# Attention blocks and norms ordered behind the in-projection products that are emitted ahead of them, and a longer counted time from transposes to values

## The chip, the cores and the metric

The kernel runs on one core of one Trainium2 chip. The metric is the device time of one execution in microseconds, the median of several runs. For the kernel before, three runs took 3193.33, 3194.68 and 3197.3 us, so the time before is 3194.68 us.

## The reference, cut to what matters

A trunk of two layers over 1024 frames of width 1024, in f32. Layer 0 mixes with RWKV-7 and gated DeltaNet heads and isn't touched by the change. Layer 1 mixes with chunked softmax attention of 16 heads of 64: each chunk of 64 frames attends to itself and the 8 chunks before it, with a bias by relative distance. Each layer ends with a squared-ReLU MLP and a gated per-layer embedding.

```python
qkv = (h @ w_qkv).reshape(bsz, seq, 3, C_HEADS, C_HEAD_DIM)
q = rmsnorm(qkv[:, :, 0], q_g) * (C_HEAD_DIM ** -0.5)
k = rmsnorm(qkv[:, :, 1], k_g)
...
s = jnp.einsum('bqhd,bkhd->bhqk', q_c, k_b).astype(jnp.float32) + bias
s = jnp.where(valid, s, -jnp.inf)
prob = jax.nn.softmax(s, -1).astype(v.dtype)
return jnp.einsum('bhqk,bkhd->bqhd', prob, v_b)
```

## The kernel before, in words

Matrices are kept as a high part and a remainder (the "split": ScalarE copies the high part in a rounded f32 type, VectorE subtracts to get the remainder), and products of high and low parts are summed on TensorE.

Attention is cut into 16 **steps**: 8 pairs of heads (pr) by 2 halves of 512 frames (hf). A step has four parts, each written as a Python generator that emits instructions and yields between them:

- `attn_in` (L1666), driven by `attn_ins` (L1597): four **in-projection products** into one of the two "dps" banks of PSUM, each of 24 matmuls of 384 columns (`dps<-wq`), three per `yield 0`. Each bank is copied out by ScalarE (qk at L1699, vs at L1703) and VectorE (vs at L1704). Then GpSimd squares (L1711), VectorE sums (L1712), takes a reciprocal square root in short instructions (L259 to L264) and scales q and k (L1715). When the 16 steps' products are out, the same generator goes on with the per-layer embedding's projection and with the output projection (`ple_proj`, `out_early`).
- `attn_norm` (L1718), driven by `attn_norms` (L1633): **norm transposes** of k and of q (`dps<-ident,qk`, L165, into "dps" banks), each followed by gains and split (L1737 to L1740).
- `attn_block` (L1745), four per step (2 heads by 2 blocks of 256 queries), driven by two copies of `attn_lane` (L1645) that draw from one list of jobs. A **block** makes for each of its two rows of queries a near score into one of two "sn" banks and a far score into the one "sf" bank; VectorE adds the bias and takes the maximum (L1795, L1803), ScalarE exponentiates (L1805, L1808) and scales by the reciprocal of the sum (L1812). Then it transposes the probabilities into one of two "pt" banks (L165), splits them into ptile (ScalarE L317, VectorE L318), and multiplies by the values into "po" (`po<-ptile,vs`). For each piece the value product with the high part comes first and that with the remainder second.

All four generators go through `run` (L123). It keeps a clock of its own, `now`, that matmuls and transposes advance (L151, L163), and for each generator a due time. It always resumes the first generator in its list that is due. A generator that yields a key such as "attn_block3" is due again after the time that the table `LAT` gives the key (L81 to L84); one that yields a tuple waits until another has marked it. The list is: two lanes, the norms, the in-projection. So the in-projection is resumed when nothing ahead of it in the list is due: it is the **filler**. It may run at most three steps ahead of the blocks (L1601).

What `run` makes is an order of emission. The framework then schedules: each engine's instructions are placed by priority (the order of emission) and by readiness in its own model of time, so an instruction that was emitted later can be placed ahead of one that the model holds to be not ready yet. The placed order of each engine is fixed in the program; on the chip each engine runs it in that order, with semaphores where it needs another engine's result.

Of the kernel before, what the change touches and what calls it, by code (L numbers as in the profile page):

```python
# [80 lines left out]
    "attn_block0": 0.97,  # L81
    "attn_block1": 4.45,
    "attn_block2": 0.43,
    "attn_block3": 0.94,  # L84
    "qk": 11.25,
    "norm": 1.28,
    "end_front": 46.33,
# [17 lines left out]
class Trunk:  # L105
    def __init__(self, ctx, tc, a, dbg=None, stop=None):
# [3 lines left out]
        self.now, self.done, self.lat = 0.0, {}, LAT  # L110
        self.nd, self.rx, self.late, self.extra = -1, None, None, []

    def dump(self, name, ap, idx=None):
        if name in self.dbg:
            d = self.dbg[name]
            d = d if idx is None else d[idx]
            self.nc.sync.dma_start(out=d, in_=ap)
# [2 lines left out]

    def run(self, lanes):  # L123
        state, self.done = [[g, 0.0, None] for g in lanes], {}
        while state:
            best = None
            for st in state:
                if st[2] is not None:
                    if st[2] not in self.done:
                        continue  # L130
                    st[1], st[2] = max(st[1], self.done[st[2]]), None
                if st[1] <= self.now:
                    best = st
                    break
                if best is None or st[1] < best[1]:
                    best = st
            self.now = max(self.now, best[1])
            try:
                r = next(best[0])
            except StopIteration:  # L140
                state.remove(best)
                continue
            if isinstance(r, tuple):
                best[2] = r
            else:
                best[1] = self.now + self.lat.get(r, 0.0)
# [4 lines left out]
    def mm(self, out, lhsT, rhs, start, stop):  # L151
        n, m = 1, 1
        for c in rhs.shape[1:]:
            n *= c
        for c in lhsT.shape[1:]:
            m *= c
        if rhs.dtype == F32:
            self.now += 2 * max(n / 1200, m * 0.0007)
        else:
            self.now += max(n / 2400, m * 0.00035)  # L160
        return self.nc.tensor.matmul(out, lhsT, rhs, start=start, stop=stop)  # L161

    def tr(self, out, in_, ident):  # L163
        self.now += 0.107
        return self.nc.tensor.transpose(out, in_, ident)  # L165

    def bank(self, shape=None):

# [1407 lines left out]
    def layer1_in(self):  # L1576
        nc, tc, a = self.nc, self.tc, self.a
        with ExitStack() as es:
            self.psm = es.enter_context(self.pool("psml1", space=PSUM))
            wp = self.wp = es.enter_context(self.pool("l1a", 2))  # L1580
            self.wr = es.enter_context(self.pool("l1wr", 2))
            self.w1 = es.enter_context(self.pool("l1w1"))
            l1 = es.enter_context(self.pool("l1", 2))
            self.sm = es.enter_context(self.pool("sml1", 2))
            self.yd = [[self.dr.tile([P, HB], F32, tag=f"yd{k}{hf}", name="yd") for hf in range(2)] for k in range(NK)]
            rbl = l1.tile([P, 16], F32, tag="rbl", name="rbl", bufs=1)
            nc.sync.dma_start(out=rbl, in_=a["rb_last"].rearrange("(o c) -> o c", o=1).broadcast_to((P, 16)))

            steps = [(pr, hf) for pr in range(8) for hf in range(2)]
            self.st = {}  # L1590

            self.ql = [[pool.tile([P, HB], F32R, tag=tag, name="Ql", bufs=1) for pool, tag in
                        ((self.accp, f"acc{e}"), (l1, f"Ql{e}"))] for e in range(2)]
            jobs = iter([(s, h, b) for s in range(16) for h in range(2) for b in range(2)])
            self.run([self.attn_lane(steps, jobs, l1, rbl) for _ in range(2)] + [self.attn_norms(steps, l1), self.attn_ins(steps, l1)])

    def attn_ins(self, steps, l1):  # L1597
        kv = {}
# [355 lines left out]
```

## Time and profile before

| what | us |
|---|---|
| median of 3 runs | 3194.68 |
| the profiled execution | 3200.01 |
| its span, first to last instruction | 3198.3 |
| layer 0 up to its dense stages | 0 to 969 |
| dense stages of layer 0 | 969 to 1770 |
| attention, products of the in-projection | 1770 to 2278 |
| attention's last blocks beside the next projections | 2278 to 2395 |
| dense stages of layer 1 | 2395 to 3198 |

The stages are read off the chain that ended last and the timeline. In the rows, PE is TensorE's matmul, PEld its weight load, DVE VectorE, ACT ScalarE, POOL GpSimd and SP SyncE, which issues the DMAs. A row of the timeline gives start, time from the first start to the last end, engine, line, operation, tiles (out<-in), shape and count of like instructions that follow each other; in brackets is the idle time of the engine just ahead, and what ended it. Matmuls overlap, so the time of one is read from start to start.

### The profile page before, as it was taken

To read this page: it belongs to the slowest core of one execution; us is meant where nothing else is said; L and a number is where in the kernel's file an instruction comes from. 1 tells how busy PE (TensorE), PEld (TensorE's weight loads), DVE (VectorE), ACT (ScalarE), POOL (GpSimd) and SP (SyncE) were. 2 spreads that over 40 slices of the span, in tenths; PEclk is the share of its full clock that TensorE was granted. 3 is DMA by queue.
4 is the path that set the end of the run, shared out by engine and by line. 5 is a ranking of instruction groups with operands and counts; after the bars stand their busy time and mean duration, and the time that the engine had idled before them with its cause. 6 is when DMAs were issued, how large, how long until landed. Compare 5 with 4: busy or idle time off the path is not lost.

```text
span 3198.3 us, 46044 instructions
## 1 busy us (share of the span) xinstructions
PE 3102.1 (97%) x17576; PEld 2565.6 (80%) x17576; DVE 2013.2 (63%) x4020; ACT 1384.2 (43%) x2608; POOL 531.5 (17%) x978
## 2 busy tenths in 40 slices
PE   7999999999999999999999898999899999999999
PEld 5777777777777888888888888988778888888887
DVE  6566675556748666655546576776768666655552
ACT  4333333334326555322123477777756555312121
POOL 6334442433410000000004211010110000000002
PEclk8999899999899999999999999999999999999999
DMA  3322112212325433523213210110156433522213
GB/s 120 94 63 60 47 46 67 70 61 70 129 95 194 155 119 108 192 93 106 92 51 128 70 36 32 45 41 16 69 177 209 150 121 109 185 105 92 106 47 105
DMA packets 144716, 309.60 MB, mean 97 GB/s; under 512 B 40944, under 2 KB 43120, under 8 KB 144496
## 3 DMA queue, kind: packets, MB, share of 16 engines
q1 hardware_dynamic: 126064, 273.10, 25.6%
q10 hardware_dynamic: 18432, 33.56, 2.7%
q8 instruction: 138, 2.26, 0.3%
q14 instruction: 82, 0.67, 0.1%
HBM read 232.16 MB, written 74.45 MB: 96 GB/s over the span
## 4 chain that ended last, share of the span: by engine, by line
PE 85%; DVE 7%; ACT 3%; DMA 2%; issue 1%; POOL 0%; SPq 0%; ACTq 0%; DVEq 0%; POOLq 0%
PE dps L161 70%; PE ch L161 3%; PE iz L161 2%; PE pm L161 2%; PE tp L161 1%; PE po L161 1%; PE py L161 1%; DVE ptile L318 1%; PE pt L165 1%; DMA wraw<-in_w_qkv 1%; PE sn L161 1%; PE pp L161 1%; DVE pb L1795 1%; PE sc L161 1%; ACT pb L1808 1%
## 5 line engine op out<-in xcount | busy, mean ns | idle before, releaser
L161 PE MATMUL dps<-r,act 128*128 128x512 f32 x3528 | 824.4, 392 | 0.0
L161 PEld LDWEIGHTS dps<-r,act 128*128 128x128 f32 x3528 | 662.1, 188 | 145.7
L161 PE MATMUL dps<-xg,whi 128*128 128x512 f32 x1280 | 438.2, 418 | 11.7 <-ACT xg L320 7.3
L161 PE MATMUL dps<-late,act 128*128 128x512 f32 x1536 | 352.9, 391 | 0.0
L161 PEld LDWEIGHTS dps<-late,act 128*128 128x128 f32 x1536 | 288.4, 188 | 63.1
L161 PE MATMUL dps<-wq,act 128*128 128x384 f32 x1536 | 304.8, 344 | 5.8 <-DVE vs L1704 3.1
L1452 POOL TENSOR_TENSOR pn<-pn,prs 128x512 f32<-128x512 f32 x32 | 45.5, 1426 | 1590.7 <-ACT prs L354 1496.3
L161 PEld LDWEIGHTS dps<-xg,whi 128*128 128x128 f32 x1280 | 248.4, 199 | 75.2 <-issue 10.7
L161 PEld LDWEIGHTS dps<-wq,act 128*128 128x128 f32 x1536 | 265.6, 191 | 10.4 <-DVE vs L1704 5.1
L161 PE MATMUL dps<-xg,wlo 128*128 128x512 f32 x640 | 266.4, 416 | 3.1 <-DVE wlo L277 3.1
L1328 DVE TENSOR_TENSOR late<-late,dps 128x512 f32<-128x512 f32 x224 | 152.9, 685 | 150.1 <-PE dps L161 119.2
L1427 DVE TENSOR_TENSOR xw<-xw,dps 128x512 f32<-128x512 f32 x192 | 131.5, 685 | 148.4 <-PE dps L161 145.5
L1226 ACT CAST act<-act 128x1024 fp32r<-128x1024 f32 (+1 forms) x99 | 94.8, 964 | 285.2 <-DMA act<-in_w 124.2
L1226 ACT CAST act<-late 128x512 fp32r<-128x512 f32 x210 | 124.5, 618 | 135.9 <-PE dps L161 117.0
L1227 DVE TENSOR_TENSOR act<-late,act 128x512 fp32r<-128x512 f32 x210 | 139.9, 687 | 26.1 <-ACT act L1226 25.9
L161 PEld LDWEIGHTS dps<-xg,wlo 128*128 128x128 f32 x640 | 126.9, 198 | 34.1 <-issue 4.8
L161 PE MATMUL dps<-xw,act 128*128 128x512 f32 x576 | 138.9, 392 | 0.0
L276 ACT CAST whi<-wraw 128x1024 fp32r<-128x1024 f32 x78 | 81.7, 1047 | 124.2 <-PE dps L161 74.4
L161 PEld LDWEIGHTS dps<-xw,act 128*128 128x128 f32 x576 | 108.1, 188 | 24.1
L1227 DVE TENSOR_TENSOR act<-act 128x1024 fp32r<-128x1024 f32 (+1 forms) x99 | 109.9, 1115 | 21.0 <-ACT act L1226 19.8
L161 PE MATMUL po<-ptile,vs 128*128 128x256 f32 (+1 forms) x576 | 104.9, 297 | 17.1 <-DVE ptile L318 7.7
L277 DVE TENSOR_TENSOR wlo<-wraw,whi 128x1024 fp32r<-128x1024 f32 x78 | 101.4, 1301 | 25.6 <-ACT whi L276 25.6
(472 smaller groups left out, 5369.4 us busy)
## 6 DMA issues: line engine op xcount, KB each, us to landing
act<-in_w SPq DMA_DIRECT2D x68, 512.0 KB
hd<-late ACTq DMA_DIRECT2D x128, 256.0 KB
late<-in_w SPq DMA_DIRECT2D x60, 512.0 KB
wraw<-in_w_in SPq DMA_DIRECT2D x56, 512.0 KB
act<-hd SPq DMA_DIRECT2D x56, 512.0 KB
wraw<-in_w_out SPq DMA_DIRECT2D x21, 512.0 KB
wraw<-in_w_qkv SPq DMA_DIRECT2D x21, 512.0 KB
pn<-pnd SPq DMA_DIRECT2D x32, 256.0 KB
```

What stands on the lines that cost most here:

```text
L161: return self.nc.tensor.matmul(out, lhsT, rhs, start=start, stop=stop)
L165: return self.nc.tensor.transpose(out, in_, ident)
L276: nc.scalar.copy(hi, raw)
L277: nc.vector.tensor_tensor(lo, raw, hi.bitcast(F32), op=ALU.subtract)
L318: nc.vector.tensor_tensor(dst[:, 1, sl], src, dst[:, 0, sl].bitcast(F32), op=ALU.subtract)
L1226: A.copy(hi, s)
L1227: V.tensor_tensor(lo, s, hi.bitcast(F32), op=ALU.subtract)
L1328: V.tensor_tensor(r, t, u, op=ALU.add)
L1427: V.tensor_tensor(x[n][:, sl], x[n][:, sl], ps, op=ALU.add)
L1452: G.tensor_tensor(pn, pn, prs[:, sl], op=ALU.mult)
L1795: V.tensor_tensor_reduce(S, pn[:, 0:nn * P], toep[:, (3 - nn) * P:], op0=ALU.add, op1=ALU.max, scale=1.0, scalar=NEG, accum_out=mx[:, 0:1])
L1808: A.activation(S, S, AF.Exp, bias=mx[:, 2:3], accum_out=l[:, 0:1])
```

## The change

Two edits. The table's time for "attn_block3", the yield between a block's last transposes and its value products, goes from 0.94 to 2.20. And `run` gets a flag, `behind`, that is set for attention alone. With it, every time a generator other than the last in the list (the filler) is resumed, the first matmul or transpose that it emits gets an edge to the last matmul that the filler has emitted: the scheduler may not place it ahead of that one. The edge is an order on TensorE itself and adds no semaphore. The filler's own instructions get no edge.

```diff
-    "attn_block3": 0.94,
+    "attn_block3": 2.20,
...
+        self.filled, self.step = None, "free"
...
-    def run(self, lanes):
+    def run(self, lanes, behind=False):
         state, self.done = [[g, 0.0, None] for g in lanes], {}
+        filling, self.filled = lanes[-1] if behind else None, None
...
             self.now = max(self.now, best[1])
+            self.step = "free" if not behind else "fill" if best[0] is filling else "tie"
             try:
                 r = next(best[0])
             except StopIteration:
                 state.remove(best)
                 continue
+            finally:
+                self.step = "free"
...
-        return self.nc.tensor.matmul(out, lhsT, rhs, start=start, stop=stop)
+        return self.placed(self.nc.tensor.matmul(out, lhsT, rhs, start=start, stop=stop))
+
+    def placed(self, ins):
+
+        if self.step == "fill":
+            self.filled = ins
+        elif self.step == "tie" and self.filled is not None:
+            self.tc.add_manual_dep(ins.ins, self.filled.ins.name, mybir.DependencyInfo(
+                mybir.DependencyClass.NoSync, mybir.DependencyReason.DATA), reason="order")
+            self.step = "tied"
+        return ins
...
-        return self.nc.tensor.transpose(out, in_, ident)
+        return self.placed(self.nc.tensor.transpose(out, in_, ident))
...
-            self.run([self.attn_lane(steps, jobs, l1, rbl) for _ in range(2)] + [self.attn_norms(steps, l1), self.attn_ins(steps, l1)])
+            self.run([self.attn_lane(steps, jobs, l1, rbl) for _ in range(2)] + [self.attn_norms(steps, l1), self.attn_ins(steps, l1)],
+                     behind=True)
```

## The prediction, made before the changed kernel ran

> **What bounds the kernel now.** I read the page's busy times first, then its chain, then the stages, then the waits of the one stage that the diff can reach.
>
> ```profile
> span 3198.3 us, 46044 instructions
> PE 3102.1 (97%) x17576; PEld 2565.6 (80%) x17576; DVE 2013.2 (63%) x4020; ACT 1384.2 (43%) x2608; POOL 531.5 (17%) x978
> ...
> PE 85%; DVE 7%; ACT 3%; DMA 2%; issue 1%; POOL 0%; SPq 0%; ACTq 0%; DVEq 0%; POOLq 0%
> ```
>
> TensorE is busy 97% of the span and is 85% of the chain that ended last. So only two things can move the time: gaps between matmuls, and the speed at which they run. The change touches the attention part of layer 1 alone, so the next view cuts the span by stage (time, PE, PEld, DVE, ACT, POOL busy, then the granted clock).
>
> ```profile
> 969.00:1770.00 801.00, 794.29 (x3478) 651.01 (x3478) 507.43 (x672) 307.74 (x467) 49.43 (x34) 0.99 0.36 124
> 1770.00:2278.00 508.00, 469.81 (x2939) 443.71 (x2940) 347.06 (x1136) 355.47 (x843) 56.70 (x64) 0.97 0.11 34
> ```
>
> In the dense stage ahead of it TensorE idles 6.7 us of 801. In attention it idles 508.00 - 469.81 = 38.2 us, with VectorE and ScalarE busy 68% and 70%: three engines hand work around, and TensorE runs out of something ready. The waits of TensorE in that stage and the tail of it (waiter, whom it waited for, total us, times, longest):
>
> ```profile
> PE po L161 <- DVE ptile L318: 7.7, 12, 1.6
> PE po L161 <- ACT ptile L317: 6.4, 10, 1.8
> PE dps L161 <- POOL acc L1465: 5.6, 1, 5.6
> PE pt L165 <- ACT pb L1812: 6.1, 9, 1.8
> PE pt L165 <- DVE ptile L318: 4.8, 12, 1.0
> PE sf L161 <- ACT pb L1805: 3.8, 7, 1.3
> PE dps L161 <- DVE vs L1704: 3.1, 6, 0.8
> ...
> PE dps L161 <- DVE F L1740: 1.8, 4, 0.5
> PE dps L165 <- DVE vs L1704: 1.7, 5, 0.5
> ```
>
> The largest family is the split of the transposed probabilities: value products wait for ptile (7.7 + 6.4), and new transposes wait until the split has emptied their bank (4.8), 18.9 us in all. Next come the transposes that wait for normalised probabilities (6.1), the two "dps" banks (3.1 + 1.8 + 1.7 = 6.6) and the one "sf" bank (3.8). The 5.6 us of acc is the start of the stage and lies ahead of the change. Where the waits sit shows in the timeline:
>
> ```profile
> 2081.28 0.55 PE L161 MATMUL po<-ptile,vs 128*128 128x128 f32 x3 [0.30 <-DVE ptile L318]
> 2081.67 0.63 PE L165 MATMUL pt<-ident,pb 128*128 128x128 f32 x4
> 2083.27 0.44 PE L165 MATMUL pt<-ident,pb 128*128 128x128 f32 x2 [0.97 <-DVE ptile L318]
> ...
> 2085.16 2.18 PE L161 MATMUL po<-ptile,vs 128*128 128x256 f32 x9 [0.92 <-DVE y L1854]
> 2087.14 0.63 PE L161 MATMUL sn<-F,F 128*128 128x384 f32 x1
> 2087.57 0.52 PE L161 MATMUL sn<-F,Ql 128*128 128x384 f32 x1
> ...
> 2098.17 3.57 PE L161 MATMUL dps<-wq,act 128*128 128x384 f32 x19
> ```
>
> From 2078.5 to 2098.2 no in-projection product runs: the blocks have only each other to hide behind. In this stretch three waits stand within 4 us, and right after them the matmuls slow down. The granted clock of such 25 us slices (third figure from the end):
>
> ```profile
> 1875.00:1900.00 25.00, 21.98 (x132) 19.72 (x132) 16.56 (x59) 20.56 (x54) 0.38 (x1) 0.93 0.03 11
> 1950.00:1975.00 25.00, 22.82 (x142) 21.33 (x141) 16.44 (x53) 18.46 (x45) 1.04 (x1) 0.93 0.03 11
> 1975.00:2000.00 25.00, 21.89 (x134) 20.69 (x133) 17.55 (x60) 17.95 (x42) 3.43 (x3) 0.93 0.06 19
> 2075.00:2100.00 25.00, 21.48 (x120) 19.19 (x119) 18.28 (x69) 17.56 (x48) 2.43 (x3) 0.80 0.16 53
> 2150.00:2175.00 25.00, 21.58 (x131) 19.25 (x129) 16.93 (x66) 17.97 (x47) 1.04 (x1) 0.93 0.16 53
> ```
>
> These five lose 25 x (4 x 0.07 + 0.20) = 12 us of clock. So the stage gives away about 38 + 12 = 50 us, 1.6% of the time, and that is all the change has to win.
>
> **The change, part by part.** No instruction is added or taken away, and no semaphore: the new edges only order TensorE's own instructions. Built, the two programs hold the same instructions on every engine. On TensorE the order is the same for the first 8,380 of 15,134 instructions and for the last 3,487; ScalarE, VectorE, GpSimd and SP also differ only inside attention. The diff alone doesn't tell the new order (a scheduler has the last word), so I counted in the two built orders. For a wait what matters is its **cover**: the TensorE work that stands between the matmul that starts a chain on the other engines and the matmul that needs its result. I price it from full-clock rows:
>
> ```profile
> 1850.02 0.36 PE L161 MATMUL sn<-F,F 128*128 128x384 f32 x1
> 1850.21 0.34 PE L161 MATMUL sn<-F,Ql 128*128 128x384 f32 x1
> ...
> 1851.64 4.43 PE L161 MATMUL dps<-wq,act 128*128 128x384 f32 x24
> 1855.91 0.28 PE L161 MATMUL sf<-F,F 128*128 128x256 f32 x1
> 1856.03 0.28 PE L161 MATMUL sf<-F,Ql 128*128 128x256 f32 x1
> ```
>
> Start to start, a product is 4.27 / 24 = 0.178 us, a 384-column score 0.19, the small ones 0.11 to 0.12 (I take 0.11).
>
> (1) *Transposes to values.* The later due time of attn_block3 (0.94 to 2.20) lets the lanes emit about 1.3 us more of products between a block's transposes and its values, and the new edges keep the scheduler from pulling the values ahead of them. The split costs at least
>
> ```profile
> L317 ACT CAST ptile<-pt 128x512 fp32r<-128x512 f32 (+2 forms) x117 | 57.2, 515 | 22.0 <-PE pt L165 21.0
> L318 DVE TENSOR_TENSOR ptile<-pt,ptile 128x512 fp32r<-128x512 f32 (+2 forms) x117 | 67.7, 594 | 11.2 <-ACT ptile L317 10.0
> ```
>
> 0.52 + 0.59 = 1.11 us, and more where it queues. Of the 144 splits, the cover up to the first value product that needs the low half is under 2.0 us 56 times before and 36 times after; what is missing to 2.0 us sums to 39.6 us before and 26.7 after. The ratio is 0.67 there, 0.67 with 1.5 us and 0.68 with 2.5 us, so it doesn't hang on the chain's length. The 18.9 us become 12.8: **-6.1 us**.
>
> (2) *Banks and normalised probabilities.* With block steps spread behind the products, the same count gives for the "dps" banks (chain taken as 2.0 us) 16.7 missing before and 8.9 after, half of 6.6: **-3.3**; it would be no gain at all if the chain were 3 us (39.4 and 39.9). For "sf" (2.0 us) 4.9 and 2.7: 45% of 3.8, **-1.7**. For the way from scores to transposes (5 us) 19.0 and 8.3: 56% of 6.1, **-3.4**. Sum of (1) and (2): -14.5 us of 38.2.
>
> A check by another count: the stretches of over 4 us of priced work without a product are 11 before (64.8 us, longest 10.3) and 10 after (51.6, longest 5.7). The longest, priced 10.3, took 19.6 us in the timeline above, 0.9 us lost per us. The 13.2 us fewer are then worth 12 us, waits and clock together: the same size.
>
> (3) *The clock.* If the halvings follow the waits, 14.5 / 38.2 = 38% of 12 us go: **-4.5**. The Trainium skill ("TensorE: Matmul & The Clock Gate", HAM oscillation) puts the rule as no idle gaps of TensorE over about 3.4 us. No wait here is that long (longest 1.8), and yet the clock halved, so the trace doesn't agree with it as a bound on single gaps; by that rule the term would be 0 and the forecast 4.5 us later. (A later section of that page names frequent short idles as another way to oscillation, which is nearer to these rows.)
>
> (4) *Norm transposes, moved forward.* This is what the change can cost. The transposes of q and k wait for a chain: copy, squares on GpSimd, sums, rsqrt, and a multiply on VectorE. Before, they stand behind 19 products of the next step; after, they stand ahead of them, at the end of the stretch without products. Seven of the sixteen have priced cover of 8.2 to 9.3 us (8.6 on average) instead of 12.0 to 13.8. Two of these in the trace, each the last product, the multiply and the transposes:
>
> ```profile
> 2107.36 4.43 PE L161 MATMUL dps<-wq,act 128*128 128x384 f32 x24
> ...
> 2121.33 1.23 DVE L1715 TENSOR_TENSOR qk<-qk,nn 128x1024 f32<-128x1024 f32 x1
> 2125.28 0.60 PE L165 MATMUL dps<-ident,qk 128*128 128x128 f32 x4
> 2246.72 1.72 PE L161 MATMUL dps<-wq,act 128*128 128x384 f32 x9
> 2256.69 1.23 DVE L1715 TENSOR_TENSOR qk<-qk,nn 128x1024 f32<-128x1024 f32 x1
> 2261.95 0.60 PE L165 MATMUL dps<-ident,qk 128*128 128x128 f32 x4
> ```
>
> The chain ended 2122.56 - 2111.79 = 10.8 and 2257.92 - 2248.44 = 9.5 us after the last product, with 2.7 and 4.0 us to spare. Against 8.6 us it would be late by 2.2 and 0.9, some 11 us over seven steps. But the cover is priced without waits; the stretch inside it loses time of its own (5.3 us at 0.9 per us is some 4 us more), and VectorE's order puts the multiply earlier too. Bounds: 0, and 11. I take **+2.5**, near the lower end, because cover in real time exceeds the chain.
>
> (5) *DMAs.* SP keeps its loads in nearly the same sequence; at the end of attention two loads of output weights now stand behind the last store of y, which waits for a block. Two whole dense products of the tail (48 matmuls) lie between that block's end and the first use of those weights, so I cost it at 0; without that cover it is one load as the chain shows it:
>
> ```profile
> 2343.75 6.11 DMA wraw<-in_w_out
> ```
>
> some 6 us.
>
> Sum: -6.1 - 3.3 - 1.7 - 3.4 - 4.5 + 2.5 = **-16.5 us**. The profiled execution took 3200.01 us (span 3198.3), so 3183.5 there; it was 5.3 us over the median of 3194.68, and the forecast for the median is **3178.2 us**.
>
> **The rivals.** (A) *The clock stays as it was*, by (3): 3182.7. For it: halving needs a stretch of waits, and ten such stretches remain. Against: the longest is almost halved. (B) *More than the listed waits go.* Gaps that each count under 0.15 us aren't in the list, and breaking the 10.3 us stretch may end its halving (0.80 in that slice) wholly: twice the forecast, 3162; the end is all 32.6 us of waits after the start and all 12 of clock, 3150. (C) *The waits move to the "dps" banks*: two banks, and blocks now can't pass a product that waits for one. With a 3 us chain (2) loses its 3.3; at 4 us the missing cover rises from 74.4 to 85.9 us. At 2 us, 16.7 us missing were 6.6 us waited, 40%; 40% of 11.5 is 4.6 lost instead of 3.3 gained. With the halvings kept: 3182.7 + 7.9 = 3190.6. Against: the copies out of a bank are three short instructions. (D) *Slower: the norm transposes hold TensorE up.* They now stand ahead of the products, so a late multiply stops everything behind it. The place is the seven steps with 8.6 us; the 19.0 us gained in (1) to (3) are eaten once 7 x (chain - 8.6) exceeds 19, a chain of 11.3 us. At 13 us, 7 x 4.4 = 31 less 19 is 12 slower: 3207. For it: 10.8 us was seen. Against: the chain had slack there, so nothing hurried it. (E) *The change does nothing*: the built orders differ, so this is only left as gains and losses that cancel, 3195.
>
> **How the numbers follow.** Forecast 0.47, A 0.18, B 0.17, C 0.08, D 0.08, E 0.02. This measurement can tell about 0.2% (6.4 us) from no change. Forecast, A and B are faster by more than that: 0.82; C and E within it: 0.10; D slower: 0.08. The range reaches from 3160, just past B's middle, to 3195, past C: it leaves out half of B and all of D.
>
> **What would show it.** Waits on ptile (18.9) near 13; po and pt the families that shrink; no stretch without products over 12 us; fewer slices under 0.95 of clock; TensorE idle near 24 us for the stage; dense stages unchanged. A new row "dps L165 <- DVE qk" of over 5 us would be D's sign, a growing "dps <- DVE vs" C's. I am wrong if the ptile waits stay at 18.9, or if they go and the time doesn't.

## The result, and the profile after

The changed kernel is slower: 3246.01 us (median of 4 runs, 3242.72 to 3246.91) against 3194.01 us (4 runs, 3190.1 to 3197.3), a ratio of 1.0161 [1.0144, 1.0179]. The forecast was 3178.2 us with a range of 3160 to 3195; the time lies 52 us above the time before and 51 us above the range. The profiled execution took 3242.72 us. All ratios are of fast executions; of the ten of e8 below, one of 3816.74 us, at a granted clock of 0.738, isn't counted in its ratio.

The head of the changed kernel's page, then its stages (start and end, length, busy time of PE, PEld, DVE, ACT and POOL, granted clock, DMA share, GB/s):

```profile
span 3241.0 us, 46056 instructions
...
PE 3116.5 (96%) x17576; PEld 2587.6 (80%) x17576; DVE 2016.6 (62%) x4020; ACT 1384.2 (43%) x2608; POOL 528.6 (16%) x978
```

```profile
969.00:1770.00 801.00, 793.80 (x3487) 652.75 (x3486) 507.71 (x678) 303.50 (x461) 53.62 (x40) 0.99 0.35 123
1770.00:2320.00 550.00, 484.24 (x2948) 464.33 (x2946) 350.44 (x1142) 359.41 (x856) 51.24 (x58) 0.92 0.09 31
...
2440.00:3241.00 801.00, 795.90 (x3486) 651.55 (x3484) 477.93 (x655) 286.15 (x432) 21.70 (x16) 1.00 0.34 123
```

The instructions on the engines are the same in number. The 12 more of the span (46056, 46044 before) are semaphore instructions that the new order needs, so the change isn't free of semaphores altogether. The dense stages are as they were. The stage of in-projection products, counted from 1770 us on, now takes 550 us where it took 508, with TensorE idle for 550.00 - 484.24 = 65.8 us (38.2 before), and the granted clock is 0.92 where it was 0.97. The same view over the whole of attention, from its first product to the last value product, for before and then for after:

```profile
1757.70:2395.30 637.60, 583.49 (x3547) 538.81 (x3548) 440.52 (x1365) 438.50 (x1015) 86.36 (x86) 0.97 0.18 60
```

```profile
1749.00:2437.50 688.50, 604.49 (x3545) 565.71 (x3546) 443.26 (x1365) 438.50 (x1016) 83.64 (x86) 0.92 0.16 56
```

Attention takes 688.5 - 637.6 = 50.9 us longer, about the loss of 52 us between the medians. (The two profiled spans differ by 42.7 us only: the part ahead of attention, which the change leaves alone, happened to be 8.7 us shorter in this execution of the changed kernel, 1749.0 us against 1757.7, with 109.2 us of it at half the granted clock against 126.3.) 21.0 us of the 50.9 is TensorE busy for longer with the same instructions (604.49 - 583.49), which I read as the clock; 29.9 us is idle time (84.0 against 54.1). VectorE and ScalarE do the same work in the same busy time. What TensorE waits for in attention, in the changed kernel (its lines stand 6 to 17 further down: L161 is now L167, L165 L181, L317 and L318 L333 and L334, L1740 L1757, L1812 L1829):

```profile
PE pt L181 <- ACT pb L1829: 17.9, 16, 3.0
PE dps L167 <- DVE F L1757: 15.2, 10, 4.4
PE po L167 <- ACT ptile L333: 10.7, 13, 2.4
PE po L167 <- DVE ptile L334: 6.0, 6, 1.5
PE dps L181 <- DVE mx L1824: 5.1, 5, 1.0
PE dps L167 <- ACT sq L1527: 4.2, 4, 1.7
PE dps L167 <- POOL act L1529: 3.8, 2, 2.6
PE pt L181 <- DVE ptile L334: 2.9, 8, 0.5
PE sf L167 <- ACT pb L1822: 2.2, 3, 1.0
PE dps L181 <- DVE vs L1721: 1.6, 2, 0.8
PE dps L181 <- DVE qk L1732: 1.6, 4, 0.5
PE dps L167 <- DVE vs L1721: 1.5, 2, 0.8
```

Two rows grew most. "dps <- DVE F" went from 1.8 to 15.2 us: an in-projection product waits for a "dps" bank, and the last to use that bank were not earlier products but the norm transposes, whose gains and split read it (F, L1757). "pt <- ACT pb" went from 6.1 to 17.9 us: transposes of probabilities wait for ScalarE to scale them. (The rows of sq and act belong to the projection behind the products; they went from 2.5 to 8.0 us together, and are still 6.3 us in e8 below, where the loss is gone.) One step boundary shows both. TensorE, ScalarE and VectorE there, in the changed kernel:

```profile
2034.69 1.09 PE L181 MATMUL dps<-ident,qk 128*128 128x128 f32 x8 [1.03 <-DVE mx L1824]
...
2036.62 0.44 PE L181 MATMUL pt<-ident,pb 128*128 128x128 f32 x2 [0.18 <-ACT pb L1829]
2040.07 0.77 PE L181 MATMUL pt<-ident,pb 128*128 128x128 f32 x5 [3.02 <-ACT pb L1829]
2042.36 4.18 PE L167 MATMUL dps<-wq,act 128*128 128x384 f32 x12 [1.52 <-DVE F L1757]
```

```profile
2037.25 0.19 ACT L1825 ACTIVATION_READ_ACCUMULATOR pb<-pb,mx 128x1 f32 x1
2037.34 0.67 ACT L1754 ACTIVATE F<-dps,vecs 64x512 fp32r<-64x512 f32 x1
2037.91 0.67 ACT L1754 ACTIVATE F<-dps,d_qg 64x512 fp32r<-64x512 f32 x1
2038.59 0.68 ACT L1756 ACTIVATE F<-dps,d_qg 64x512 fp32r<-64x512 f32 x1
2039.30 1.41 ACT L1829 ACTIVATE pb<-pb,l 128x512 f32<-128x512 f32 x3
2040.74 0.68 ACT L1754 ACTIVATE F<-dps,vecs 64x512 fp32r<-64x512 f32 x1
```

```profile
2034.30 0.34 DVE L1721 SCALAR_TENSOR_TENSOR vs<-dps,rscol,vs 128x128 fp32r<-128x128 f32 x1
2034.56 0.14 DVE L1824 TENSOR_SCALAR mx<-mx 128x1 f32<-128x1 f32 x1
...
2038.04 0.74 DVE L1757 SCALAR_TENSOR_TENSOR F<-dps,vecs,F 64x512 fp32r<-64x512 f32 x1 [0.41 <-ACT F L1754]
2039.31 0.74 DVE L1757 SCALAR_TENSOR_TENSOR Ql<-dps,d_qg,F 64x512 fp32r<-64x512 f32 x1 [0.52 <-ACT F L1756]
2041.45 0.76 DVE L1757 SCALAR_TENSOR_TENSOR F<-dps,vecs,F 64x512 fp32r<-64x512 f32 x1 [1.40 <-ACT F L1754]
```

At 2034.69 all eight norm transposes, of k and of q, run one after another and fill both "dps" banks. (They had waited 1.03 us themselves. The row names mx, which is no operand of theirs; the copy of vs out of a "dps" bank ended just ahead of them, at 2034.64, so I read the row of mx, 5.1 us in all, as waits for that bank.) ScalarE first ends the exponentials of a block (to 2037.44), and only then makes the first gain copies. VectorE splits the first half of k from 2038.04 on. ScalarE's queue then holds the scaling of probabilities (L1829) behind three gain copies, so TensorE's transposes wait 3.02 us for it; the second half of k is copied behind that scaling and split by 2042.21. Only then is the bank of k free, 6.4 us after the last of the eight transposes ended, and the product that waited for it starts at 2042.36. Between the two waits TensorE had 0.77 us of work, and nothing to fill them with: the fillers themselves need the two banks.

The granted clock of three such 25 us slices of the changed kernel:

```profile
1875.00:1900.00 25.00, 18.28 (x104) 16.76 (x103) 15.12 (x48) 16.26 (x40) 1.04 (x1) 0.86 0.10 33
1950.00:1975.00 25.00, 19.43 (x103) 17.91 (x102) 15.23 (x48) 17.24 (x43) 1.54 (x1) 0.80 0.11 39
2025.00:2050.00 25.00, 18.27 (x106) 16.75 (x105) 15.21 (x47) 17.09 (x42) 1.04 (x1) 0.86 0.12 44
```

They come back in nearly every step: 19 of the 26 slices from 1775 to 2425 lie under 0.95, where 6 of 25 did before. Summed over attention, the records grant half the clock for 116.1 us, against 41.0 before (a mean clock of 0.92 over 688.5 us is 2 x 0.08 x 688.5 = 110).

Why the banks? Both built orders were counted again, by one distance alone: the priced work between a norm transpose and the next product in the same bank. In the order of emission, with the later due time, the norm transposes come ahead of the next step's products, and the edges keep them there; before, 19 of the next product's 24 matmuls mostly stood first. Places with under 3 us of such cover: 0 before, 15 after. And the time that a bank is held, from the last transpose to the last read, is a mean of 5.4 us for k and 6.5 for q in the trace of before, 6.3 and 7.5 in that of after. So the banks were held nearly as long before; what is new is that a product wants one of them so soon. The short places are those of k's bank.

### The profile page after: what moved, and what is told of

Read it like the earlier page. It is cut to its first block, busy times and chain, and to the rows that moved or that the text cites. A ratio compares the mean times of both kernels' runs of the same rounds, so it can differ in the third digit from the quotient of the medians.

```text
span 3241.0 us, 46056 instructions
## 1 busy us (share of the span) xinstructions
PE 3116.5 (96%) x17576; PEld 2587.6 (80%) x17576; DVE 2016.6 (62%) x4020; ACT 1384.2 (43%) x2608; POOL 528.6 (16%) x978
## 3 DMA queue, kind: packets, MB, share of 16 engines
q1 hardware_dynamic: 126064, 273.10, 24.6%
## 4 chain that ended last, share of the span: by engine, by line
PE 87%; DVE 6%; ACT 4%; issue 1%; DMA 1%; POOL 0%; SPq 0%; DVEq 0%; ACTq 0%; POOLq 0%
PE dps L167 71%; PE ch L167 3%; PE iz L167 2%; PE po L167 2%; PE pm L167 2%; PE tp L167 1%; PE py L167 1%; PE sn L167 1%; PE pt L181 1%; PE pp L167 1%; ACT pb L1825 1%; ACT F L1754 1%; ACT pb L1829 1%; PE sc L167 1%; DVE ptile L334 1%
## 5 line engine op out<-in xcount | busy, mean ns | idle before, releaser
L167 PE MATMUL dps<-r,act 128*128 128x512 f32 x3528 | 824.4, 392 | 0.0
L167 PEld LDWEIGHTS dps<-r,act 128*128 128x128 f32 x3528 | 662.2, 188 | 145.6
L167 PE MATMUL dps<-xg,whi 128*128 128x512 f32 x1280 | 433.4, 414 | 11.2 <-ACT xg L336 7.4
L167 PE MATMUL dps<-wq,act 128*128 128x384 f32 x1536 | 335.9, 364 | 17.7 <-DVE F L1757 15.0
L167 PE MATMUL dps<-late,act 128*128 128x512 f32 x1536 | 352.9, 391 | 0.0
L167 PEld LDWEIGHTS dps<-late,act 128*128 128x128 f32 x1536 | 288.5, 188 | 63.1
L167 PEld LDWEIGHTS dps<-wq,act 128*128 128x128 f32 x1536 | 289.9, 206 | 21.4 <-issue 14.2
L167 PEld LDWEIGHTS dps<-xg,whi 128*128 128x128 f32 x1280 | 245.5, 196 | 73.4 <-issue 10.7
L167 PE MATMUL dps<-xg,wlo 128*128 128x512 f32 x640 | 263.8, 412 | 3.1 <-DVE wlo L293 3.1
L167 PEld LDWEIGHTS dps<-xg,wlo 128*128 128x128 f32 x640 | 125.2, 196 | 33.6 <-issue 4.8
L167 PE MATMUL dps<-xw,act 128*128 128x512 f32 x576 | 138.9, 392 | 0.0
L167 PEld LDWEIGHTS dps<-xw,act 128*128 128x128 f32 x576 | 108.1, 188 | 24.1
L167 PE MATMUL po<-ptile,vs 128*128 128x256 f32 (+1 forms) x576 | 103.5, 292 | 19.0 <-ACT ptile L333 10.7
```

What stands on the lines that cost most here:

```text
L167: return self.placed(self.nc.tensor.matmul(out, lhsT, rhs, start=start, stop=stop))
```

## The experiments

Three theories were set against each other. **Banks**: norm transposes pinned ahead of products hold both "dps" banks while ScalarE and VectorE read them in turn, and products, and through ScalarE's queue the blocks, wait behind. **Edges**: the edges cost by themselves, since no block step can pass a late product any more. **Due time**: the later due time alone does it. The columns: ratio to the kernel before with its 95% interval, median, length of attention (from its first product to its last value product, which holds 3504 matmuls in e1 to 3584 in e10, 3546 in before and 3544 in after, so that lengths compare only to some 10 us), TensorE's idle times of over 0.15 us summed, time at half the granted clock, and places with under 3 us of cover behind the norm transposes (those of the kernels that copy the banks out mean little, since the bank is then free early).

| kernel | ratio | us | attention | idle | half clock | places |
|---|---|---|---|---|---|---|
| before | | 3194.01 | 637.6 | 51.1 | 41.0 | 0 |
| after | 1.0161 [1.0144, 1.0179] | 3246.01 | 688.5 | 83.0 | 116.1 | 15 |
| e1_time_only | 1.0022 [1.0008, 1.0035] | 3205.87 | 640.4 | 53.8 | 68.3 | 2 |
| e2_edges_only | 0.9996 [0.9983, 1.0010] | 3194.99 | 634.8 | 55.4 | 47.8 | 2 |
| e3_norms_spread | 1.0099 [1.0076, 1.0122] | 3231.03 | 669.6 | 71.7 | 88.7 | 9 |
| e4_norms_ptbank | 1.0035 [1.0019, 1.0050] | 3211.62 | 649.7 | 58.0 | 85.3 | |
| e5_pinned_early | 1.0333 [1.0314, 1.0351] | 3301.31 | 732.8 | 119.1 | 170.7 | 13 |
| e6_edges_130 | 1.0074 [1.0054, 1.0094] | 3221.43 | 664.8 | 67.9 | 92.2 | 7 |
| e7_edges_190 | 1.0074 [1.0058, 1.0090] | 3219.62 | 660.5 | 61.8 | 81.9 | 8 |
| e8_bank_copied_out | 1.0001 [0.9983, 1.0019] | 3198.88 | 639.6 | 56.6 | 54.6 | |
| e9_before_copied_out | 0.9986 [0.9972, 0.9999] | 3190.74 | 627.6 | 53.6 | 54.6 | |
| e10_k_bank_copied_out | 1.0004 [0.9993, 1.0015] | 3197.78 | 642.6 | 54.2 | 47.8 | |
| e11_copied_190 | 0.9972 [0.9959, 0.9984] | 3186.85 | 628.4 | 54.2 | 47.8 | |
| e12_copied_130 | 0.9985 [0.9973, 0.9997] | 3190.54 | 632.9 | 49.3 | 54.6 | |

The medians of the kernel before beside them were 3197.54 (e1 to e4), 3195.31 (e5 to e8) and 3197.6 (e9 to e12).

**e1_time_only and e2_edges_only**: each edit by itself. e1 is the kernel before with the later due time; e2 is the changed kernel with the old one.

```diff
-    "attn_block3": 0.94,
+    "attn_block3": 2.20,
```

> The table's 2.20 alone, no edges. Theory banks (the later due time lets the norm transposes come due ahead of the next step's products, the edges pin them there, their gain copies hold both dps banks for 6 to 7 us and the products wait): the scheduler may still pull products ahead, the cover missing between norm transposes and the next product in their bank is near that of before, so 3190 to 3205. Theory edges (order alone, blocks that may not pass a waiting product): 3194. Theory due time (a longer gap ahead of the values uses up products and leaves longer stretches without): 3230 to 3250.

```diff
-    "attn_block3": 2.20,
+    "attn_block3": 0.94,
```

> The edges alone, due time 0.94. Theory banks: at 0.94 the norm transposes come due behind the next step's first product, so the edges pin a good order: 3180 to 3200. Theory edges: most of the 52 us is here, 3225 to 3250. Theory due time: 3194.

Measured: +0.2% (3205.87 us, 0.9 above what "banks" expected) and no difference. Neither "edges" nor "due time" holds alone; of these two edits the loss needs both. The first waits of e2 in attention are the old ones:

```profile
PE po L167 <- DVE ptile L334: 9.3, 11, 1.5
PE pt L181 <- ACT pb L1829: 8.0, 9, 1.8
```

and e1 shows the wait for the bank begin (1.8 before), with the scheduler still free to place products ahead of the transposes:

```profile
PE dps L161 <- DVE F L1740: 5.8, 8, 1.9
```

**e3_norms_spread**: both edits; the transposes of k (of steps 2 to 14) wait in the emission for the next step's first product, those of q for its second, so that no two fill both banks together.

```diff
             # attn_in, behind the copies of a product
+            self.mark(("pd", 2 * pr + hf, e))
             # attn_norm, ahead of its bank
+            if 2 <= s < 15:
+                yield ("pd", s + 1, 1 - j)
```

> Both edits, but the k transposes of steps 2 to 14 wait until the next step's first product has been emitted, the q transposes until its second. Theory banks: at least half of the loss comes back, 3195 to 3220, and TensorE's wait of dps products for F (15.2 us) falls under 6. Theories edges and due time: 3235 to 3255, since neither is touched.

Measured 1.0099, 3231.03 us, which is in the range of no theory: about two fifths of the loss went, but the wait for the bank grew, where under 6 us was expected. So the time doesn't follow this one row. Its first wait:

```profile
PE dps L167 <- DVE F L1760: 24.4, 8, 4.3
```

In the built order every second step still had the transposes right ahead of a product (9 places). The edit moved the place, and didn't free the bank; it is no test of what a free bank is worth.

**e4_norms_ptbank**: both edits; the norm transposes take a "pt" bank in place of a "dps" bank.

```diff
-            pt = self.bank()
+            pt = self.psm.tile([P, HB], F32, tag="pt", name="npt", bufs=2)
```

> Both edits, but the norm transposes go into the two pt banks instead of the two dps banks. Theory banks: the wait of products for F disappears, and comes back in part as transposes of probabilities that wait for a pt bank; 3205 to 3240, half-speed clock less than the 106 us of the changed kernel. Theories edges and due time: 3240 to 3255.

Measured 1.0035: the products' wait for F is gone, and with it four fifths of the loss. (The expectation's 106 us of half-speed clock are counted in the 25 us slices from 1775 us on; over the whole of attention it is 116.1.) What the rest is stays open: the first two waits are for ptile and for scaled probabilities, and transposes of probabilities wait only 2.1 us for a "pt" bank that holds norm transposes:

```profile
PE po L167 <- ACT ptile L333: 10.7, 10, 3.4
PE pt L181 <- ACT pb L1829: 8.6, 9, 1.8
...
PE pt L181 <- DVE F L1757: 2.1, 1, 2.1
```

**e5_pinned_early**: edges with the old due time, and the products of a step wait in the emission for the norm transposes of the step before, which pins them at the same place without the later due time.

```diff
             # attn_ins, ahead of a step's products
+                yield ("nm", s - 1)
             # attn_norms, behind attn_norm
+            self.mark(("nm", s))
```

> Edges with the old due time 0.94 (alone worth nothing, 0.9996), plus one wait in the emission: the products of a step come only after the norm transposes of the step before it. Theory banks: pinning the norm transposes ahead of products is enough, 3225 to 3265, with TensorE's wait of dps products for F over 12 us and half-speed clock over 90 us. Theory due time (the loss needs 2.20): 3190 to 3205.

Measured 1.0333 (3301.31 us), slower than after and outside the ranges of both theories. "Banks" expected products to wait over 12 us for F; with 13 places of short cover they wait only 2.5 us. So short cover alone doesn't make that wait; here TensorE is held up by others first:

```profile
PE dps L181 <- DVE qk L1734: 24.6, 9, 4.2
PE po L167 <- DVE y L1873: 20.0, 7, 4.3
```

This is the prediction's rival D: transposes pinned so early that their own chain is late. It shows that D's mechanism exists, with 24.6 us in its row, and that it isn't what happened in the changed kernel, where that row is 1.6 us. As a test of the banks it isn't clean.

**e6_edges_130 and e7_edges_190**: the changed kernel with other due times.

```diff
-    "attn_block3": 2.20,
+    "attn_block3": 1.30,
```

> Edges with a due time of 1.30. In the built order 7 places (15 in the changed kernel, 0 before) have under 3 us of priced work between norm transposes and the next product in their bank, and the cover of the value products is as good as in the changed kernel. Theory banks: between, 3185 to 3215. Theory due time (loss grows with the time): 3205 to 3215, a quarter of the loss.

```diff
-    "attn_block3": 2.20,
+    "attn_block3": 1.90,
```

> Edges with a due time of 1.90. 8 such places of under 3 us, cover of the value products better than in the changed kernel (22.0 us missing to 2 us, 26.7 there). Theory banks: like e6, 3185 to 3220. Theory due time: three quarters of the loss, 3230 to 3240.

Both measured 1.0074, with 7 and 8 places: between e2 (2 places, 0.9996) and after (15, 1.0161), in the order of the places. e6, at 3221.43 us, is over the ranges of both theories; e7, at 3219.62, is within that of "banks". But not by the bank's wait alone: in e6 products wait 12.6 us for banks with norm transposes, in e7 only 4.3 us, and other waits come first there:

```profile
PE sf L167 <- ACT pb L1822: 11.4, 12, 2.1
...
PE dps L167 <- DVE F L1757: 4.3, 6, 1.9
```

**e8_bank_copied_out and e9_before_copied_out**: the hold itself. VectorE copies the 512 columns of both norm banks to SBUF at once, and gains and split read the copy. e8 is the changed kernel with it, e9 the kernel before with the same copy, as the control.

```diff
             # attn_norm, ahead of the loop over the gains
+            sc = self.wp.tile([P, HB], F32, tag="sq", name="nsc", bufs=1)
+            nc.vector.tensor_copy(sc, pt)
+            pt = sc
```

> The changed kernel, but VectorE copies each bank of norm transposes into SBUF first and the gains and splits read the copy, which adds 32 copies of about 0.6 us on VectorE. Priced cover between norm transposes and products stays short (14 places under 3 us). Theory banks: the bank is free after some 1 to 3 us instead of 6 to 7, the wait of products for F goes, at least half of the loss comes back, 3195 to 3225. Rival (the stop is the wait for probabilities behind a loaded ScalarE, not the bank): 3240 to 3265, since no work leaves ScalarE and VectorE gets more.

> Control for e8: the kernel before with the norm banks copied out by VectorE. Theory banks: there the products hardly wait for F (1.8 us), so freeing the banks early wins little and 32 more copies cost little, 3185 to 3205. If the copy wins by itself 40 us or more here (3155 or less), e8 told nothing of the change.

Measured 1.0001 and 0.9986. 32 copies, added to VectorE's work, take back the whole loss of about 52 us; on the kernel before they are worth about 0.14%, at the edge of what the interval can tell. The copies in e8 (count, then ns from least to most), and what is left of the wait for the bank:

```profile
L1754 DVE COPY nsc<-dps x32: 679/692/693, 1803.8 to 2302.0; 128x512 f32<-128x512 f32 x32
```

```profile
PE pt L181 <- ACT pb L1832: 15.2, 14, 2.1
...
PE dps L167 <- DVE nsc L1754: 1.4, 3, 0.8
```

From the last transpose to the end of the copy, k's bank is now held for a mean of 1.4 us and q's for 4.5, where it was 6.3 and 7.5. (The copy itself is 0.69 us; the two copies share one buffer in SBUF, which q's finds taken by k's.) ScalarE's gain copies are no shorter from the copy (0.72 us, 0.68 from the bank), so what helps isn't less work on ScalarE. The scaled probabilities are waited for nearly as long as in after (15.2 against 17.9), but no longer in one piece of 3 us, and seldom behind gain copies: such copies are among the five ScalarE instructions ahead of the scaling for 2.1 us of it, for 13.8 us in after. The time at half clock is 54.6 us instead of 116.1.

**e10_k_bank_copied_out**: the changed kernel, copying k's bank alone.

```diff
+            if j:
+                sc = self.wp.tile([P, HB], F32, tag="sq", name="nsc", bufs=1)
+                nc.vector.tensor_copy(sc, pt)
+                pt = sc
```

> The changed kernel with only the bank of the k transposes copied out, the one that the next product takes; q's bank stays held. Theory banks, the first product's wait being the larger part: 3195 to 3220. If q's bank held matters as much: 3220 to 3240. Rival (loaded ScalarE): 3240 or more.

Measured 1.0004: k's bank alone carries the loss. It is the first that a product needs; q's is still held for a mean of 7.2 us here. Its waits on ptile are now below the 12.8 us that the prediction gave for the change (5.5 + 3.3 = 8.8 us, none of the third row):

```profile
PE pt L181 <- ACT pb L1833: 10.3, 10, 1.8
...
PE po L167 <- ACT ptile L333: 5.5, 13, 0.7
...
PE pt L181 <- DVE ptile L334: 3.3, 10, 0.7
PE dps L167 <- DVE Ql L1761: 3.2, 3, 1.7
```

**e11_copied_190 and e12_copied_130**: the copies of e8 with e7's and e6's due times.

```diff
-    "attn_block3": 2.20,
+    "attn_block3": 1.90,
...
+            sc = self.wp.tile([P, HB], F32, tag="sq", name="nsc", bufs=1)
+            nc.vector.tensor_copy(sc, pt)
+            pt = sc
```

> Edges, due time 1.90, both norm banks copied out: the order with the best cover of the value products (23.0 us missing to 2 us, against 37.0 in e9). Theory banks, with step (1) of the prediction kept: 3175 to 3195, faster than both kernels. If cover of the values is worth little: 3195 to 3205, as e8.

```diff
-    "attn_block3": 2.20,
+    "attn_block3": 1.30,
...
+            sc = self.wp.tile([P, HB], F32, tag="sq", name="nsc", bufs=1)
+            nc.vector.tensor_copy(sc, pt)
+            pt = sc
```

> Edges, due time 1.30, both norm banks copied out: missing cover of the values 26.4 us, fewest stretches without products but one of 11.4 us. Theory banks with step (1) kept: 3175 to 3195. If cover is worth little: 3195 to 3205.

Measured 0.9972 and 0.9985. e11 is faster than both kernels, by some 9 us to the kernel before; its interval overlaps that of e9 (0.9972 to 0.9999), so how much of that the edges and the due time bring beside the copy isn't settled. Its waits:

```profile
PE pt L181 <- ACT pb L1832: 11.4, 10, 2.0
...
PE po L167 <- DVE ptile L334: 3.9, 5, 1.9
PE po L167 <- ACT ptile L333: 3.7, 8, 0.6
PE pt L181 <- DVE ptile L334: 3.1, 8, 0.7
```

"Banks" stands, then, for the changed kernel: the loss goes when the bank is copied out, all of it, in two kernels (e8 and e10), while the short places stay. It takes both: the bank held for long, as in before (5.4 us for k) and in e1 (6.2), neither of which shows the loss, and a product that wants it soon. Left open: e7's loss, where products wait only 4.3 us for such banks and which yet goes with the copy (the copy also changes the built order there); and how the 50.9 us divide between waits and clock as causes, which was read off the windows and not separated by a run.

## Why the prediction was wrong

**(1) Transposes to values, -6.1 us: the wait can be taken away by about that much, but no time came of it.** The waits on ptile are 6.0 + 10.7 + 2.9 = 19.6 us after, 18.9 before, and the forecast 12.8. With the norm banks free they are 12.6 (e8), 8.8 (e10), 10.7 (e11) and 12.4 (e12), against 23.1 in the control e9. So more cover does shorten these waits; in the changed kernel the rows are full again, beside ScalarE's late copies and a halved clock. But with the due time alone (e1) they are 11.2 us, and e1, e8 and e10 are no faster than the kernel before. In e8 TensorE is idle for 56.6 us in all, 51.1 before, since other rows grew: "pt <- pb" to 15.2 us, "sf" to 7.2. In these kernels that is the prediction's own last sign of being wrong, waits that go while the time doesn't: it took each row's shrinking as time gained, and the idle time came back in another row. Only e11 leaves room for a gain.

**(2) Banks, -3.3 us: this step failed.** It counted every use of a "dps" bank with one chain of 2.0 us, which is about what the copies behind a product take (a median of 2.1 us in the trace of before). The norm transposes use the same banks, and there the chain for k is two gain copies on ScalarE and two splits on VectorE one after the other, 0.67 + 0.74 + 0.67 + 0.76 = 2.8 us of work (q has two gain copies more). The trace of before would have shown the bank held for 3.2 us at the shortest, and a mean of 5.4 us for k and 6.5 for q. The prediction had the counts that turn the sign (39.4 to 39.9 us at 3 us, 74.4 to 85.9 at 4 us), and gave them a rival's 8%. Counted by itself, to 4 us, the cover missing from a norm transpose to the next product in its bank goes from 5.5 to 28.5 us; the wait went from 1.8 to 15.2. The two smaller terms: "sf" went from 3.8 to 2.2 us, about as forecast (-1.7); "pt <- pb", forecast at -3.4, went up by 11.8, and for most of it the scaling on ScalarE now stands close behind gain copies (13.8 us of 17.9, as against 1.6 of 6.1 before).

**(3) The clock, -4.5 us: the other way.** It was tied to the waits, and the two did move together: waits up, and the time at half clock from 41.0 to 116.1 us. The Trainium skill ("TensorE: Matmul & The Clock Gate", HAM oscillation) gives single idle gaps of over about 3.4 us as the bound. In the changed kernel one wait behind the start of attention is longer (4.4 us), and 19 slices are under 0.95, so as a bound on single gaps the trace doesn't bear it out; the following section of that page, on frequent short idles, fits these rows better.

**(4) Norm transposes ahead of the products, +2.5 us: this step failed too, though not in the wait that it priced.** That wait, for the chain of qk, is 1.6 us. But the moved transposes also wait for a bank: with the row of mx read as above, their rows are 1.6 + 1.6 + 5.1 = 8.3 us, against 1.7 before, 6.6 more. And above all the step asked what the transposes wait for, and not what waits for them: as users of a bank they hold up the products, by 15.2 us, and through ScalarE's queue the blocks. Rival D named the right place and the wrong direction, and its sign (over 5 us in the row of qk) didn't come; e5 shows it where it does. Rival C named the right resource, and had the holder half wrong: the two rows of vs went from 4.8 to 3.1 us, with mx to 8.2, and the 15.2 us are not for copies of products but for the norms' own.

**(5) The DMAs at 0** agree: from the last value product to the end it is 803.5 us, 803.0 before, and TensorE's waits for weights of the projections behind (wq) went from 1.2 us to none.

The cross-check, stretches without products, couldn't catch the miss: it priced TensorE's own work, and in the changed kernel the stretch from 2034.69 to 2042.36 holds about 3 us of work and 4.7 us of waits.

Two smaller slips changed nothing in the outcome. With the new order the program has 12 more semaphore instructions, where none was expected. And rival B's end took the 5.6 us of acc out of the 38.2 us of idle time a second time: that wait ended at 1770.22, so the stage from 1770 on holds only 0.2 us of it.

## What to carry to other kernels

When an instruction is moved ahead of others, price both directions: what it waits for, and how long it keeps the buffer that the next ones need, read per user of that buffer from the timeline (from the write to the last read on any engine), never with one figure for a shared pool. Where two engines read a PSUM bank in turn and one of them has a queue, a copy to SBUF ahead of them can be a cheap fix: 0.69 us of VectorE each, 32 times, took back 52 us, and 16 of them, for the one bank that is wanted soon, did as much. Don't add up rows of waits as time to be won: what leaves one row can come back in another, as the idle time of e8 shows. And if a sum's sign turns within the bounds of one duration, measure that duration in the trace before choosing the forecast.

## What the runs showed of the hardware that was not expected

The granted clock halves beside clusters of waits that are short by themselves. In attention the records grant half the clock in 7 stretches before and in 18 in the changed kernel, each of 3.41 us or a multiple of it up to 13.65; the longest wait behind the start is 1.8 us before and 4.4 in the changed kernel, and only that one is over 3.41.

The time at half clock goes with the time that the same number of matmuls keeps TensorE busy. Over the first 3600 from attention's first product on, it is 41.0 us at half clock and 596.1 busy of 650.2 (before), 68.3 and 606.7 of 662.8 (e1), 88.7 and 606.4 of 679.5 (e3), 116.1 and 617.6 of 701.6 (after), 170.7 and 633.1 of 753.3 (e5): 0.2 to 0.4 us of busy time for each us more at half clock. Half clock alone doesn't set the length: e4, with 85.3 us at half clock and 603.0 us busy, is close to e3 in both, but takes 662.2 us, 17.3 less, and 13.9 of that is idle time. No run changes the clock with the waits kept, so which share of the loss each causes stays open.
